# A gate's last dot products, a residual load by halves and a provisional mean in a two-layer hybrid block

## Chip, cores and metric

One core of one Trainium2 chip runs the whole block. The metric is the device time of one execution in microseconds (us); the kernel before has a median of 2440.19 us over three runs (2438.97 to 2441.34).

## What is computed

Two layers over 1024 latent tokens of width 1024 (stored as 8 tiles `d` of 128 channels). Layer 0 mixes tokens with a bidirectional RG-LRU (ten channel tiles of 128), layer 1 with a Conformer convolution module. Each layer ends in a gated ConvFFN, and every sub-layer is normed, modulated by adaLN and added to the residual h. Cut from the reference:

```python
mod = s_c @ ada_w[i] + ada_b[i]
sh1, sc1, g1, sh2, sc2, g2 = [t[:, None, :] for t in jnp.split(mod, 6, axis=-1)]
h = h + g1 * rglru_out(hf + hb, ug, w_out)          # layer 0
h = h + g1 * conformer_conv(xm, ...)                # layer 1
h = h + g2 * conv_ffn(xm2, w_up, cw, cb, w_down)    # both layers

def conformer_conv(xm, w1, b1, cw, cb, lng, lnb, w2, b2):
    a, g = jnp.split(xm @ w1 + b1, 2, axis=-1)
    v = dwconv1d(a * jax.nn.sigmoid(g), cw, cb, (15, 15))
    mu = v.mean(-1); var = ((v - mu) ** 2).mean(-1)
    return jax.nn.silu((v - mu) * rsqrt(var + EPS) * lng + lnb) @ w2 + b2

def conv_ffn(xm, w_up, cw, cb, w_down):
    v, g = jnp.split(dwconv2d(xm @ w_up, cw, cb), 2, axis=-1)
    return (jax.nn.silu(g) * v) @ w_down
```

## The kernel before

**Products and order.** Every fp32 product is made of three TensorE matmuls of a high and a low part: weights are split into `whi` (ACT) and `wlo` (mostly POOL), activations into `xmh`/`zh` (ACT) and `xml`/`zl` (DVE or POOL). A class `Order` is a list scheduler: it holds predicted durations (`dur`), a priority (`prio`, smaller first) and a sequence number, and writes one instruction order for each engine, which is then fixed; an engine runs its list strictly in that order. PE's order is the order in which the program issues matmuls. DMAs are issued by SP, in its own order, from one queue.

**Layer 0's output projection** (`rnn_out`, L1021; `k_outer`, L942). It goes by token half `hf` (512 tokens). For each half it runs over k, the ten tiles of the recurrence's output; for each k all eight output tiles d get three matmuls into eight PSUM banks. The last two k (8 and 9, `tail`) are done tile by tile with the residual add (`finish`). Each k needs a weight tile `wraw<-w_out_in` of 512 KB, with a split, and z, which `rnn_feed` reads back from DRAM (`raw<-ydr`) and `z_split` splits. During k = 4 to 7 of half 0, `load_h` (L1415) loads h, two tiles of 512 KB at each k, through the same queue.

**Layer 0's ConvFFN** (`ffn`, L1078). 22 steps p each make two column tiles of the up-projection on PE, in three PSUM pairs P0 to P2 in turn. For each tile ACT writes the centre tap and DVE adds the other eight (`ffn_conv`, `cv<-ps,vec,cv`): 16 taps, one gate product and so on per step. z of step p goes to POOL for its low part (`zl`). From p = 3 on `between()` puts a unit of the down-projection into PE's stream every four k steps: 12 matmuls into P3, then DVE adds `h<-ps,mod,h` with the gate g2 (`self.modB[l][5]`), which frees P3 for the next unit.

**The gate.** g2 of layer 0 is part 5 of `mod[0]`, eight columns, each a dot product of a row of `ada_w` with silu(c) (`ada_dot`, L543). The product of a 512 KB row tile in the two-buffer ring `raw` with `sC` is done by DVE with an accumulated sum, or by POOL with a sum on ACT. `first_tiles` issues four DVE dots at p = 0 (`prio=3`), p = 1 and p = 2 issue two POOL dots each, and then `ada_bias(0, 5)` adds the bias (`mod<-mod,vec`). `ada_dot` with a `prio` lets its load go early; with `prio=0` the load waits for `after`. Loads of the down weights (`raw<-down_in`) share the ring.

**The Conformer's layernorm** (`conformer`, L1215). Eight channel tiles; the odd ones are convolved on PE (`conv`). conv(7) is the last; its result goes to DRAM and back to be put in order again (`yt`, `cdr`, `sC`), and an ACT instruction writes CV tile 7. For half 0 `center(0, ...)` sums the mean on PE (POOL's running sum `nacc`, and CV tiles 5, 6 and 7), subtracts it from all eight tiles on DVE, squares on ACT, sums the variance on PE; then `rsqrt`, and `src` scales, applies SiLU and splits each tile for the second pointwise product. Half 1 is centred while half 0's product runs (`first` of `k_outer`), and its variance (`deviation`) is one matmul on `nacc` that stands in PE's stream behind k = 3.

Of the kernel before, what the change touches and what calls it, by code (L numbers as in the profile page):

```python
# [280 lines left out]
class Net:  # L281
# [258 lines left out]

    def ada_dot(self, l, q, eng="dve", after=(), prio=0):  # L543

        t, b = self.load_raw(self.a["ada"][l, q], after=() if prio else after)
        col, mB = self.mod[l][:, q:q + 1], self.modB[l][q // 8]
        if eng == "dve":
            self.stt(1024, t, t, 1.0, self.sC, MULT, MULT, [b, self.sCB], [b], [mB], accum=col, after=after, prio=prio)
        else:
            self.tten(1024, t, t, self.sC, MULT, [b, self.sCB], [b], eng=eng, prio=prio)  # L550
            self.act(1024, t, t, AF.Copy, [b], [b], [mB], accum=col)
# [349 lines left out]
    def k_outer(self, K, zsrc, flush, after_stat, pts=(0, 1, 2, 3), first=None, during={}, last=None):  # L901
# [30 lines left out]
        def outer(hf, after, ws):  # L932

            late = max(after) + 1 if after else 0
            for k in range(max(late, K - tail)):
                if K > 4:
                    ws[k] = self.w_next(min(2, 3 - k) if k < late else 2)
                for d in range(ND - 2 if k < late else ND):
                    unit(d, hf, [k], ws)
                    if d == (2 if K > 4 else 0) and k in after:  # L940
                        after[k](bank(ND - 1, hf))
                if hf == 0 and k in during:  # L942
                    during[k]()
                if k == late - 1:
                    for kk in range(late):
                        for d in (ND - 2, ND - 1):
                            unit(d, hf, [kk], ws)
                        if late == 4:
                            self.w_split(self.wq_use + min(kk + 1, 3))
            if K == 4:  # L950
                self.w_split(self.wq_use + 2)
                self.w_load(self.wq_use + 4)
            else:
                for k in range(K - tail, K):
                    ws[k] = self.w_next()
            for d in (0, 2, 4, 6, 1, 3, 5, 7):
                unit(d, hf, range(K - tail, K), ws)
                finish(d, hf)
# [53 lines left out]
    def rnn_feed(self, i):  # L1012

        while self.fed < min(i, 2 * NR):
            hf, k = divmod(self.fed, NR)
            t, b = self.yr.next()
            self.dma(t, self.ydr[k][:, hf * 512:hf * 512 + 512], 262144, r=[self.ydrB[k][hf]], w=[b])
            self.z_split(k, t, b, "dve")
            self.fed += 1

    def rnn_out(self, during):  # L1021
# [10 lines left out]
            b.w = [o for _, c in self.yr.items[2 * i:2 * i + 2] for o in c.w + c.r]  # L1032
            b.r = []

    def z_split(self, k, t, b, eng, n=512):
        i = self.zi % 8
        self.zi += 1
        hB, lB = self.xB[1][i]
        hi, lo = self.xmh[1][:, i, :], self.xml[1][:, i, :]
        self.act(n, hi, t, AF.Copy, [b], [hB])  # L1040
        self.tten(n, lo, t, hi.bitcast(F32), SUB, [b, hB], [lB], eng=eng, prio=-1)

    def z_slot(self, i):
        return self.xmh[1][:, i, :], self.xml[1][:, i, :], list(self.xB[1][i])
# [18 lines left out]
    def ffn(self, l, end, last=None):  # L1063
# [80 lines left out]
        for p in range(NF):  # L1144
# [9 lines left out]
            for q in ((), (0,), (1, 2))[p] if p < 3 else ():  # L1154
                quarter(0, q)
            if p == 0:
                self.first_tiles((0, 1), lambda ops: [self.ada_dot(*ada.pop(0), prio=3, after=ops) for _ in range(4)] if ada else None)
                pts, nt = [0, 1], 2
            for i, f in enumerate((p, NF + p)):
                if p:  # L1160
# [48 lines left out]
    def conformer(self, pool):  # L1209
# [56 lines left out]
        def glu(m, pt):  # L1266
# [12 lines left out]
            self.act(W, inner(hi), split(xr), AF.Copy, [xrB], [hB], prio=-2)  # L1279
            self.tten(W, inner(lo), split(xr), inner(hi).bitcast(F32), SUB, [xrB, hB], [lB], prio=-2)  # L1280

        def conv(m):
            hi, lo, hB, lB = xs[m // 2 % 2]
            out = self.P[3].rearrange("p a (b s) -> p (a b) s", b=2)
            slot = None
            for j in range(4):
                for n, d in enumerate(SHIFTS):
# [8 lines left out]
                            self.mm(out[:, j, :], w[:, c], x[:, j, s], n == 0 and q == 0, n == len(SHIFTS) - 1 and q == 2)  # L1296

                    o.pe(3 * (256 / 2400 + 0.011), go, [whB, wlB, hB, lB], [self.PB[3][j // 2]])
            for h in range(2):
                c = slice(512 * h, 512 * h + 512)  # L1300
                self.ts(512, yt[:, c], self.P[3][:, h, :], 1.0, None, MULT, None, [self.PB[3][h]], [yB[h]], prio=-2)
# [40 lines left out]
            for m in range(ND):  # L1342
                sums(m, *xs[m])

        var = self.P[1][:, 0, :]

        def sums(m, x, b):
            sq, sqB = self.tt.next()
            self.act(512, sq, x, AF.Square, [b], [sqB])
            o.pe(0.87, lambda: self.mm(var, self.ones, sq, m == 0, m == ND - 1), [self.onesB, sqB], [self.PB[1][0]])  # L1350

        center(0, (0, 0), sums)
        self.rsqrt(512, rs2[0][0], var, [self.PB[1][0]], [rs2[0][1]])

        def deviation(bank):
            ms = self.stat(*lna[1], bank)
# [7 lines left out]
        def src(hf, k):  # L1364
            while self.fed < min(hf * ND + k + 5, 16):
                h, m = order[self.fed]
                self.fed += 1
                c = slice(h * 512, h * 512 + 512)
                x, b = CV[:, m, c], cvB[m][h]
                self.tten(512, x, x, rs2[h][0], MULT, [b, rs2[h][1]], [b])  # L1370
                silu = self.act(512, x, x, AF.Silu, [b], [b], bias=self.v("cf_ln_b", m), scale=self.v("cf_ln_g", m))
                self.z_split(m, x, b, "dve")
# [29 lines left out]
    def build(self):  # L1402
        tc, o = self.tc, self.o
        with ExitStack() as main:
# [3 lines left out]
            def switch():  # L1408
# [1 line left out]
                o.drain()  # L1410
                ex.close()
                self.h = main.enter_context(tc.tile_pool(name="h", bufs=1)).tile([P, ND, 1024], F32, name="h")
                self.hB = []

            def load_h():  # L1415
                for d in (len(self.hB), len(self.hB) + 1):
                    both = Buf()
                    self.dma(self.h[:, d, :], self.a["x"][:, d, :], 524288, w=[both])
                    self.hB.append([Buf(after=[both]), Buf(after=[both])])

            during = {4: lambda: (switch(), load_h()), 5: load_h, 6: load_h, 7: load_h}
            for l in range(2):
                if l == 0:
                    self.rnn_out(during)
# [32 lines left out]
```

## Time and profile before

| | |
|---|---|
| median of 3 runs | 2440.19 us |
| profiled execution | 2438.16 us, span 2436.4 us (1.76 us lie around the span) |
| granted TensorE clock, mean | 0.979 |
| PE busy | 2326.2 us, 95% |
| DVE busy | 1896.6 us, 78% |
| ACT, POOL busy | 967.3 us (40%), 798.1 us (33%) |
| DMA | 214.98 MB, mean 88 GB/s |

In the profile a time is a position in the span, in us; "released by" or "<-" names the engine and tile whose end ended a wait. A matmul record is longer than the step from one to the next, since matmuls are pipelined. A granted clock of 1.0 is the 2.4 GHz level, 0.5 the 1.2 GHz level.

### The profile page before, as it was taken

To read this page: it belongs to the slowest core of one execution; us is meant where nothing else is said; L and a number is where in the kernel's file an instruction comes from. 1 tells how busy PE (TensorE), PEld (TensorE's weight loads), DVE (VectorE), ACT (ScalarE), POOL (GpSimd) and SP (SyncE) were. 2 spreads that over 40 slices of the span, in tenths; PEclk is the share of its full clock that TensorE was granted. 3 is DMA by queue.
4 is the path that set the end of the run, shared out by engine and by line. 5 is a ranking of instruction groups with operands and counts; after the bars stand their busy time and mean duration, and the time that the engine had idled before them with its cause. 6 is when DMAs were issued, how large, how long until landed. Compare 5 with 4: busy or idle time off the path is not lost.

```text
span 2436.4 us, 26124 instructions
## 1 busy us (share of the span) xinstructions
PE 2326.2 (95%) x10440; PEld 1892.8 (78%) x10440; DVE 1896.6 (78%) x1752; ACT 967.3 (40%) x1141; POOL 798.1 (33%) x409
## 2 busy tenths in 40 slices
PE   7999999889789999999999999889999999999997
PEld 2788888667578888888887888667888888888886
DVE  6677877776867777777878898677997777777878
ACT  4577777544233333333324333365322221222223
POOL 1100000354345544554523233245333322332323
PEclk9999999899899999999999999899999999999999
DMA  6324325253132323223211233422111111111101
GB/s 262 120 84 144 94 84 162 96 198 117 55 101 95 104 87 104 95 88 103 91 35 36 66 114 105 138 70 91 52 58 52 44 39 52 52 52 48 44 26 70
DMA packets 82442, 214.98 MB, mean 88 GB/s; under 512 B 8528, under 2 KB 33104, under 8 KB 82192
## 3 DMA queue, kind: packets, MB, share of 16 engines
q1 hardware_dynamic: 80448, 210.68, 26.3%
q10 hardware_dynamic: 1872, 2.62, 0.3%
q8 instruction: 82, 1.34, 0.2%
q14 instruction: 40, 0.33, 0.0%
HBM read 192.10 MB, written 13.63 MB: 84 GB/s over the span
## 4 chain that ended last, share of the span: by engine, by line
PE 70%; DVE 16%; ACT 5%; issue 3%; DMA 2%; POOL 2%; SPq 0%; ACTq 0%; DVEq 0%; POOLq 0%
PE ps L441 70%; DVE cv L362 4%; DVE CV L362 3%; DVE F L770 1%; ACT F L354 1%; POOL wlo L369 1%; DVE F L362 1%; DVE tt L362 1%; DVE F L369 1%; DVE rs L384 1%; ACT tt L354 1%; DVE raw L362 1%; ACT L354 1%; DVE h L362 1%; ACT whi L354 1%
## 5 line engine op out<-in xcount | busy, mean ns | idle before, releaser
L362 DVE SCALAR_TENSOR_TENSOR cv<-ps,vec,cv 128x960 f32<-128x960 f32 (+2 forms) x720 | 861.5, 1198 | 203.6 <-ACT cv L354 185.2
L441 PE MATMUL ps<-xmh,whi 128*128 128x512 f32 x2272 | 744.5, 394 | 19.7 <-ACT xmh L354 8.9
L441 PE MATMUL ps<-xmh,wlo 128*128 128x512 f32 x2272 | 738.0, 392 | 9.5 <-POOL wlo L369 5.9
L441 PE MATMUL ps<-xml,whi 128*128 128x512 f32 x2272 | 740.5, 393 | 4.6 <-DVE xml L362 4.2
L369 POOL TENSOR_TENSOR wlo<-wraw,whi 128x1024 fp32r<-128x1024 f32 (+1 forms) x164 | 399.8, 2442 | 712.6 <-ACT whi L354 694.9
L441 PEld LDWEIGHTS ps<-xmh,whi 128*128 128x128 f32 x2272 | 427.8, 189 | 115.9 <-ACT xmh L354 12.0
L441 PEld LDWEIGHTS ps<-xmh,wlo 128*128 128x128 f32 x2272 | 429.4, 189 | 103.1 <-POOL wlo L369 7.9
L441 PEld LDWEIGHTS ps<-xml,whi 128*128 128x128 f32 x2272 | 429.8, 189 | 102.4 <-DVE xml L362 9.4
L362 DVE SCALAR_TENSOR_TENSOR h<-ps,mod,h 128x1024 f32<-128x1024 f32 (+2 forms) x216 | 231.5, 1080 | 61.0 <-PE ps L441 60.8
L354 ACT ACTIVATE whi<-wraw 128x1024 fp32r<-128x1024 f32 (+1 forms) x198 | 205.2, 1042 | 123.3 <-PE ps L441 51.5
L354 ACT ACTIVATE cv<-ps,vec 128x1024 f32<-128x1024 f32 (+1 forms) x90 | 105.9, 1181 | 299.5 <-PE ps L441 280.5
L369 POOL TENSOR_TENSOR zl<-cv,zh 128x1024 fp32r<-128x1024 f32 x42 | 101.2, 2411 | 350.6 <-ACT zh L354 350.6
L441 PE MATMUL ps<-zh,dnh 128*128 128x512 f32 x576 | 180.1, 393 | 23.0 <-DVE h L362 23.0
L369 POOL TENSOR_TENSOR raw<-raw,sC 128x1024 f32<-128x1024 f32 x52 | 125.1, 2406 | 178.7 <-DMA raw<-ada_in 174.0
L441 PE MATMUL ps<-zl,dnh 128*128 128x512 f32 x576 | 181.4, 397 | 0.0
L441 PE MATMUL ps<-zh,dnl 128*128 128x512 f32 x576 | 177.8, 390 | 0.0
L354 ACT ACTIVATE raw<-raw 128x1024 f32<-128x1024 f32 x52 | 55.2, 1062 | 289.4 <-POOL raw L369 289.4
L354 ACT ACTIVATE cv<-cv 128x1024 f32<-128x1024 f32 (+1 forms) x46 | 47.0, 1022 | 293.5 <-DVE cv L362 293.3
L369 POOL TENSOR_TENSOR dnl<-raw,dnh 128x512 fp32r<-128x512 f32 x72 | 94.0, 1307 | 202.5 <-ACT dnh L354 202.5
L362 DVE SCALAR_TENSOR_TENSOR CV<-ps,vec,CV 128x1009 f32<-128x1009 f32 (+14 forms) x120 | 153.1, 1275 | 8.6 <-ACT CV L354 4.9
L441 PEld LDWEIGHTS ps<-zh,dnh 128*128 128x128 f32 x576 | 108.6, 189 | 45.9 <-DVE h L362 23.4
L441 PEld LDWEIGHTS ps<-zh,dnl 128*128 128x128 f32 x576 | 108.4, 188 | 26.4
(141 smaller groups left out, 2414.6 us busy)
## 6 DMA issues: line engine op xcount, KB each, us to landing
raw<-ada_in SPq DMA_DIRECT2D x88, 512.0 KB, 4.2
wraw<-up_in SPq DMA_DIRECT2D x88, 512.0 KB, 3.3
raw<-down_in SPq DMA_DIRECT2D x72, 256.0 KB, 3.2
wraw<-w_in SPq DMA_DIRECT2D x32, 512.0 KB, 3.3
wraw<-w_in_in SPq DMA_DIRECT2D x20, 512.0 KB, 3.9
wraw<-w_out_in SPq DMA_DIRECT2D x20, 512.0 KB, 3.7
wraw<-cw_in SPq DMA_DIRECT2D x16, 512.0 KB, 3.6
wraw<-gw_in SPq DMA_DIRECT2D x10, 512.0 KB, 3.4
```

Source lines behind the costliest of these rows:

```text
L354: "act", 0.21 + n * 0.00083, lambda: self.nc.scalar.activation(out, in_, func, **kw),
L362: lambda: self.nc.vector.scalar_tensor_tensor(out=out, in0=in0, scalar=scalar, in1=in1, op0=op0, op1=op1, **kw),
L369: return self.o.op(eng, dur, lambda: e.tensor_tensor(out=out, in0=in0, in1=in1, op=op), r, w, wp, prio=prio)
L384: return self.o.op("dve", 0.07 + n * 0.0063, lambda: self.nc.vector.reciprocal(out=out, in_=in_), r, w)
L441: self.nc.tensor.matmul(out, w, x, start=start, stop=stop)
L770: lambda t=t, a=a, ig=ig, rev=rev: nc.vector.tensor_tensor_scan(rev(t), rev(a), rev(ig), 0.0, op0=MULT, op1=ADD),
```

## The change

Four edits. (1) `ada_dot` takes the early load as a parameter of its own, and the four dots of `first_tiles` get `prio=0` in place of 3. (2) `load_h` loads h by token halves: 256 KB for each tile, half 0 at the same k as before, half 1 at k = 0 to 3 of half 1. (3) The first four `z_split` of `rnn_feed` get a priority of 4 (and 3 for the low part). (4) For half 0 of the Conformer's layernorm the mean of the first seven tiles is summed inside conv(7); `deviate` subtracts 8/7 of it on DVE from each tile and squares the result on ACT; when tile 7 has come back, one matmul on its deviation gives the difference d between the provisional and the true mean, the variance is corrected by d squared, and d is subtracted from every tile in `src`, one more DVE instruction per tile.

```diff
-    def ada_dot(self, l, q, eng="dve", after=(), prio=0):
-        t, b = self.load_raw(self.a["ada"][l, q], after=() if prio else after)
+    def ada_dot(self, l, q, eng="dve", after=(), prio=0, early=False):
+        t, b = self.load_raw(self.a["ada"][l, q], after=() if early else after)
...
-                if hf == 0 and k in during:
-                    during[k]()
+                if (hf, k) in during:
+                    during[hf, k]()
...
-            self.z_split(k, t, b, "dve")
+            self.z_split(k, t, b, "dve", prio=4 if self.fed < 4 else 0)
...
-                self.first_tiles((0, 1), lambda ops: [self.ada_dot(*ada.pop(0), prio=3, after=ops) for _ in range(4)] if ada else None)
+                self.first_tiles((0, 1), lambda ops: [self.ada_dot(*ada.pop(0), early=True, after=ops) for _ in range(4)] if ada else None)
...
+        def provisional():
+            parts = [lna[0], *((CV[:, m, :512], cvB[m][0]) for m in LATE[:-1])]
+            for i, (t, tB) in enumerate(parts):
+                o.pe(0.87, lambda: self.mm(self.P[0][:, 1, :], self.ones, t, i == 0, i == len(parts) - 1), [self.onesB, tB], [self.PB[0][1]])
...
+                    if m == ND - 1 and j == 3 and n == 5:
+                        provisional()
...
-        var = self.P[1][:, 0, :]
-
-        def sums(m, x, b):
+        r, rB = rs2[0]
+        d, dB = lna[0]
+        (mp, mpB), (mu, muB), (var, varB) = [(self.P[i][:, j, :], self.PB[i][j]) for i, j in ((0, 1), (0, 0), (1, 0))]
+
+        def total(out, outB, t, tB, first, last):
+            o.pe(0.87, lambda: self.mm(out, self.ones, t, first, last), [self.onesB, tB], [outB])
+
+        def deviate(m, y, yB):
+            self.stt(512, y, mp, -ND / (ND - 1.0), CV[:, m, :512], MULT, ADD, [cvB[m][0], mpB], [yB], prio=-3)
             sq, sqB = self.tt.next()
-            self.act(512, sq, x, AF.Square, [b], [sqB])
-            o.pe(0.87, lambda: self.mm(var, self.ones, sq, m == 0, m == ND - 1), [self.onesB, sqB], [self.PB[1][0]])
-
-        center(0, (0, 0), sums)
-        self.rsqrt(512, rs2[0][0], var, [self.PB[1][0]], [rs2[0][1]])
+            self.act(512, sq, y, AF.Square, [yB], [sqB], prio=-4)
+            return sq, sqB
+
+        for m in range(ND - 1):
+            total(var, varB, *deviate(m, CV[:, m, :512], cvB[m][0]), m == 0, False)
+        w, wB = vt[:, :512], vB
+        sq = deviate(ND - 1, w, wB)
+        total(mu, muB, w, wB, True, True)
+        total(var, varB, *sq, False, True)
+        sq, sqB = self.tt.next()
+        self.act(512, sq, mu, AF.Square, [muB], [sqB], prio=-4)
+        self.act(512, d, mu, AF.Copy, [muB], [dB], prio=-3)
+        self.tten(512, r, var, sq, SUB, [varB, sqB], [rB], prio=-4)
+        self.rsqrt(512, r, r, [rB], [rB])
+        inverse = list(rB.w)
...
+                if h == 0:
+                    x, b = (w, wB) if m == ND - 1 else (x, b)
+                    o.op("dve", 0.72, lambda x=x: nc.vector.tensor_tensor(out=x, in0=x, in1=d, op=SUB), [b, dB], [b], after=inverse if m else ())
...
-            def load_h():
-                for d in (len(self.hB), len(self.hB) + 1):
-                    both = Buf()
-                    self.dma(self.h[:, d, :], self.a["x"][:, d, :], 524288, w=[both])
-                    self.hB.append([Buf(after=[both]), Buf(after=[both])])
-
-            during = {4: lambda: (switch(), load_h()), 5: load_h, 6: load_h, 7: load_h}
+            def load_h(hf, d0):
+                for d in (d0, d0 + 1):
+                    c = slice(hf * 512, hf * 512 + 512)
+                    self.dma(self.h[:, d, c], self.a["x"][:, d, c], 262144, w=[self.hB[d][hf]])
+
+            during = {(hf, 4 * (1 - hf) + i): lambda hf=hf, i=i: load_h(hf, 2 * i) for hf in range(2) for i in range(4)}
+            during[0, 4] = lambda: (switch(), load_h(0, 0))
```

**The gate's dots, DVE, start of layer 0's ConvFFN.** Names: `cv<-ps,vec,cv` is a tap (or a few of one form), `raw_77,mod_92<-raw_77,sC` a dot, `mod_92<-mod_92,vec` the gate's bias, `h<-ps_68,mod_92,h` a unit's add to h. Before, where the fourth dot stands:

```order
L362 SCALAR_TENSOR_TENSOR cv_3480<-ps_66,vec,cv_3480 128x15x63 x4
L362 SCALAR_TENSOR_TENSOR cv_3481<-ps_67,vec,cv_3481 128x960 x2
L362 SCALAR_TENSOR_TENSOR cv_3481<-ps_67,vec,cv_3481 128x16x63 x2
L362 SCALAR_TENSOR_TENSOR cv_3481<-ps_67,vec,cv_3481 128x15x63 x4
L362 SCALAR_TENSOR_TENSOR raw_77,mod_92<-raw_77,sC 128x1024
L369 TENSOR_TENSOR cv_3480<-cv_3480,cv_3481 128x1024
L369 TENSOR_TENSOR mod_92<-mod_92,vec 128x8
L362 SCALAR_TENSOR_TENSOR h<-ps_68,mod_92,h 128x1024 x2
```

and now, from the third dot on:

```order
L362 SCALAR_TENSOR_TENSOR raw_76,mod_92<-raw_76,sC 128x1024
L362 SCALAR_TENSOR_TENSOR cv_3487<-ps_65,vec,cv_3487 128x960 x2
L362 SCALAR_TENSOR_TENSOR raw_77,mod_92<-raw_77,sC 128x1024
L362 SCALAR_TENSOR_TENSOR cv_3487<-ps_65,vec,cv_3487 128x16x63 x2
L362 SCALAR_TENSOR_TENSOR cv_3487<-ps_65,vec,cv_3487 128x15x63 x4
L362 SCALAR_TENSOR_TENSOR cv_3488<-ps_66,vec,cv_3488 128x960 x2
L362 SCALAR_TENSOR_TENSOR cv_3488<-ps_66,vec,cv_3488 128x16x63 x2
L362 SCALAR_TENSOR_TENSOR cv_3488<-ps_66,vec,cv_3488 128x15x63 x4
L362 SCALAR_TENSOR_TENSOR cv_3489<-ps_67,vec,cv_3489 128x960
L369 TENSOR_TENSOR cv_3487<-cv_3487,cv_3488 128x1024
L362 SCALAR_TENSOR_TENSOR cv_3489<-ps_67,vec,cv_3489 128x960
L369 TENSOR_TENSOR mod_92<-mod_92,vec 128x8
```

The fourth dot stood behind the 48 taps of the first six tiles and now stands behind two; the gate's bias stood behind all 48 and now stands behind 18, and the first two adds to h, which stood together behind it, now lie four and five tiles' taps in (not shown).

**The Conformer's layernorm, DVE, from conv(7)'s result on.** Names: `yt` is conv(7)'s result on its way to DRAM, `CV<-CV,ps_65` the old centring, `CV<-ps_65,CV` the provisional one, `nacc_89` at L1397 is d, `CV<-CV,rs` the scaling of half 0, `CV<-CV,ps_68` the centring of half 1. Before:

```order
L377 TENSOR_SCALAR yt<-ps_68 128x512 x2
L369 TENSOR_TENSOR CV<-CV,ps_65 128x512 x8
L384 RECIPROCAL rs<-rs 128x512
L369 TENSOR_TENSOR CV<-CV,rs 128x512 x4
L369 TENSOR_TENSOR xml_75<-CV,xmh_73 128x512 x2
L369 TENSOR_TENSOR CV<-CV,rs 128x512
L369 TENSOR_TENSOR xml_75<-CV,xmh_73 128x512 x3
L369 TENSOR_TENSOR CV<-CV,ps_68 128x512 x3
```

and now:

```order
L377 TENSOR_SCALAR yt<-ps_68 128x512
L362 SCALAR_TENSOR_TENSOR CV<-ps_65,CV 128x512
L377 TENSOR_SCALAR yt<-ps_68 128x512
L362 SCALAR_TENSOR_TENSOR CV<-ps_65,CV 128x512 x6
L362 SCALAR_TENSOR_TENSOR raw_76<-ps_65,CV 128x512
L369 TENSOR_TENSOR rs<-ps_66,tt 128x512
L1397 TENSOR_TENSOR CV<-CV,nacc_89 128x512
L384 RECIPROCAL rs<-rs 128x512
L369 TENSOR_TENSOR CV<-CV,rs 128x512
L1397 TENSOR_TENSOR CV<-CV,nacc_89 128x512
L369 TENSOR_TENSOR CV<-CV,rs 128x512
L1397 TENSOR_TENSOR CV<-CV,nacc_89 128x512
```

Seven centrings moved ahead of tile 7's return, one of them between the two copies of `yt`; seven of the eight subtractions of d stand behind the reciprocal, in turn with the scalings, and ahead of or among half 1's centring.

## Rows read from the trace of the kernel before

**Rows 1.** The page, part 4: the chain that ended last, by engine.

```profile
PE 70%; DVE 16%; ACT 5%; issue 3%; DMA 2%; POOL 2%; SPq 0%; ACTq 0%; DVEq 0%; POOLq 0%
```

**Rows 2.** PE's waits: line waited for, us in total, times, longest us.

```profile
PE ps L441 <- DVE h L362: 26.5, 4, 23.0
```

**Rows 3.** Windows: stretch, length, then busy us (instructions) of PE, PEld, DVE, ACT, POOL, clock, DMA share, GB/s.

```profile
650.00:660.00 10.00, 3.16 (x14) 2.27 (x13) 9.74 (x10) 1.06 (x1) 0.00 (x0) 0.81 0.00 0
660.00:670.00 10.00, 0.00 (x0) 0.00 (x0) 0.79 (x1) 2.21 (x3) 4.63 (x2) 0.50 0.28 95
670.00:680.00 10.00, 3.85 (x9) 3.07 (x10) 1.45 (x2) 3.82 (x5) 3.61 (x2) 0.50 0.26 88
680.00:690.00 10.00, 10.00 (x45) 8.17 (x45) 8.79 (x8) 1.58 (x2) 6.87 (x4) 0.99 0.51 160
```

**Rows 4.** Timeline, DVE and POOL near 600: start, length, what, count, idle before and releaser.

```profile
596.41 21.08 DVE L362 SCALAR_TENSOR_TENSOR cv<-ps,vec,cv 128x960 f32<-128x960 f32 x17
598.18 2.40 POOL L369 TENSOR_TENSOR wlo<-wraw,whi 128x1024 fp32r<-128x1024 f32 x1 [7.89 <-ACT whi L354]
```

**Rows 5.** Timeline, all engines, 650 to 678.

```profile
649.61 8.77 DVE L362 SCALAR_TENSOR_TENSOR cv<-ps,vec,cv 128x960 f32<-128x960 f32 x7
...
658.30 1.22 DVE L362 SCALAR_TENSOR_TENSOR raw<-raw,sC 128x1024 f32<-128x1024 f32 x1
```

**Rows 6.** The chain in order of time, 660 to 680: start, us, what.

```profile
667.80 3.13 DMA raw<-ada_in
...
670.99 2.35 POOL raw L369
...
674.82 1.29 DVE h L362
...
676.15 4.15 PE ps L441 x9
```

**Rows 7.** SP's issues of the four tiles of ada_w, near 575.

```profile
575.67 19.14 SPq L343 DMA_DIRECT2D raw<-ada_in  x4
```

**Rows 8.** The page, part 6, DMA issues: count, KB each, median us to landing.

```profile
raw<-ada_in SPq DMA_DIRECT2D x88, 512.0 KB, 4.2
```

**Rows 9.** Window in layer 0's output projection, columns as in rows 3.

```profile
490.00:500.00 10.00, 4.56 (x13) 2.45 (x12) 4.88 (x3) 3.15 (x4) 4.70 (x2) 0.79 1.03 406
```

**Rows 10.** SP's issues of h ahead of the last weight tile of half 0.

```profile
482.96 0.89 SPq L343 DMA_DIRECT2D h<-x_in  x2
...
484.86 1.30 SPq L343 DMA_DIRECT2D h<-x_in  x2
```

**Rows 11.** The chain in order of time, 478 to 500.

```profile
486.20 9.29 DMA wraw<-w_out_in
...
496.73 2.36 POOL wlo L369
```

**Rows 12.** Timeline, PE, in the Conformer's layernorm.

```profile
1561.45 1.02 PE L441 MATMUL ps<-nacc,ones 128*128 128x512 f32 x2
1562.31 1.88 PE L441 MATMUL ps<-CV,ones 128*128 128x512 f32 x4
...
1589.64 0.79 PE L441 MATMUL ps<-xmh,whi 128*128 128x512 f32 x1 [6.40 <-ACT xmh L354]
...
1612.26 1.12 PE L441 MATMUL ps<-nacc,ones 128*128 128x512 f32 x2 [1.88 <-POOL nacc L369]
```

**Rows 13.** Timeline, DVE, in the same stretch.

```profile
1573.05 4.87 DVE L369 TENSOR_TENSOR CV<-CV,ps 128x512 f32<-128x512 f32 x8 [10.11 <-PE ps L441]
1584.00 3.35 DVE L384 RECIPROCAL rs<-rs 128x512 f32<-128x512 f32 x1 [6.08 <-ACT rs L354]
...
1599.94 0.68 DVE L369 TENSOR_TENSOR CV<-CV,rs 128x512 f32<-128x512 f32 x1
...
1601.82 2.88 DVE L369 TENSOR_TENSOR nacc<-nacc,tt 128x512 f32<-128x512 f32 x1
```

**Rows 14.** Timeline, POOL, beside it.

```profile
1601.75 2.40 POOL L369 TENSOR_TENSOR wlo<-wraw,whi 128x1024 fp32r<-128x1024 f32 x1
```

More of the change, by code (lines that the diff above doesn't have):

```diff
@@ L1033, in rnn_out, with z_split @@
             b.r = []
-    def z_split(self, k, t, b, eng, n=512):
+    def z_split(self, k, t, b, eng, n=512, prio=0):
         i = self.zi % 8
@@ L1039, in z_split @@
         hi, lo = self.xmh[1][:, i, :], self.xml[1][:, i, :]
-        self.act(n, hi, t, AF.Copy, [b], [hB])
-        self.tten(n, lo, t, hi.bitcast(F32), SUB, [b, hB], [lB], eng=eng, prio=-1)
+        self.act(n, hi, t, AF.Copy, [b], [hB], prio=prio)
+        self.tten(n, lo, t, hi.bitcast(F32), SUB, [b, hB], [lB], eng=eng, prio=prio - 1)
     def z_slot(self, i):
@@ L1412, in switch @@
                 self.h = main.enter_context(tc.tile_pool(name="h", bufs=1)).tile([P, ND, 1024], F32, name="h")
-                self.hB = []
-            def load_h():
-                for d in (len(self.hB), len(self.hB) + 1):
-                    both = Buf()
-                    self.dma(self.h[:, d, :], self.a["x"][:, d, :], 524288, w=[both])
-                    self.hB.append([Buf(after=[both]), Buf(after=[both])])
-            during = {4: lambda: (switch(), load_h()), 5: load_h, 6: load_h, 7: load_h}
+                self.hB = [[Buf(), Buf()] for _ in range(ND)]
+            def load_h(hf, d0):
[4 more added lines that the diff above has]
+            during[0, 4] = lambda: (switch(), load_h(0, 0))
             for l in range(2):
```

## Prediction

> **What bounds the kernel now.** I read the chain of waits first. PE holds 70% of it [rows 1], so a change counts only where PE stands still or where something else ends a stretch of PE's work. The list of PE's waits then names the largest hole by far: 26.5 us in four waits for DVE's add to h, one of them 23.0 us long [rows 2]. The windows place it: PE works 3.16 us of the ten from 650, none from 660 to 670, 3.85 us from 670 to 680, and is full again after that [rows 3]. What the reader is to see in the next two views is why. DVE is full until 658 with taps (17 in 21.08 us [rows 4], 7 in 8.77 us [rows 5]: 1.24 us each), and only then comes `raw<-raw,sC` at 658.30, the fourth of the gate's early dots [rows 5]. Its data had been asked for by 594.8, as the last of the four issues that began at 575.67 and took 19.14 us [rows 7]. So the dot did not wait for data; it stood behind 48 taps in DVE's order. It holds one of the two `raw` buffers, the next loads wait for that buffer, and the rest follows one link after another: load at 667.80, POOL's product at 670.99, the sum on ACT, the gate's bias, the add to h at 674.82, PE at 676.15 [rows 6]. The second unit of the down-projection cannot enter P3 before that add has emptied it.
>
> Two smaller holes lie where the change also works: the tail of layer 0's output projection, where PE works 4.56 us of the ten from 490 [rows 9], and the Conformer's layernorm, where PE waits 6.40 us up to 1589.64 and 1.88 us up to 1612.26 [rows 12].
>
> **The change, part by part.** Edits are costed against the profiled execution, 2438.16 us, which is 2.03 us under the median of 2440.19.
>
> *The gate's dots.* Nothing is added; one dot of 1.22 us moves ahead of 46 taps. In the new order it comes after two taps, at about 596.41 + 2 x 1.24 = 598.9. Its load, issued by 594.8, lands about 4.2 us later [rows 8], near 599.0: the two meet, and DVE waits nothing or a few tenths. The dots that depend on the buffer then start some 35 us earlier; the order puts the gate's bias behind 18 taps, about 596.4 + 18 x 1.24 + 1.2 for the dot and 1.2 for a gate product = 621. The first add to h then hangs on P3 alone. I place it among the taps of the fifth tile, near 649 to 650, so the second unit enters P3 near 653, where PE stopped before. Is something else late next? DVE's backlog is the candidate. PE runs ahead of DVE by about one step: by my walk along both orders the taps of the sixth tile end near 662.4, and PE needs that bank for its ninth tile only near 672, 9.5 us later. Nearer is POOL's low part of z for the first unit: with DVE 1.2 us later it is ready near 645.75, wanted near 646.3. From step 3 on a step gives DVE about 25.5 us (16 taps, products and three or four adds) and PE about 32.7 us, so the backlog shrinks. So the whole 23.0 us goes. With it goes the slow clock behind it: from 670 to 680 the clock is 0.50, the 1.2 GHz level, and the 9 matmuls took 3.85 us; at 45 in 10.00 us [rows 3] they would take 2.0. Term: **−23.0 − 1.85 = −24.85 us**. Bounds: 0 if the gate is as late as before; the same −24.85 as the most.
>
> *h by halves.* The queue is full from 490 on (DMA share 1.03 at 406 GB/s [rows 9]). Ahead of the last weight tile of half 0, issued at 486.20, stand four h loads [rows 10]; each shrinks by 262,144 bytes, together 1.05 MB, 2.58 us at 406 GB/s. That tile's 9.29 us end at 495.49, its split on ACT and POOL follows at once and ends at 499.09 [rows 11], and PE goes on. 2.58 us sooner its split would meet POOL still busy with the tile before, but two of the four loads stand ahead of that one too, so it comes about 1.3 us sooner and POOL is free in time. I take **−2.6 us**. Bounds: 0, if the z parts that ride in the same queue end last instead; −5.4, the whole idle time of the ten us from 490 [rows 9]. The eight loads of half 1 run beside 40 us of PE's work and are wanted only by that half's adds; I cost them at nothing, and if they came late it would be those adds and the norm behind them.
>
> *Priority of the first splits.* One split on ACT changes places with four others while PE is in the recurrence; the first product needs all of them later. Nothing.
>
> *The provisional mean.* Three matmuls move into conv(7), 0.86 us each (1561.45 to 1562.31 [rows 12]), so conv(7) ends 2.58 us later, and one centring of 0.66 stands between the two copies of `yt`: tile 7 comes back 3.25 us later. Behind it there are no longer eight centrings (4.87 us [rows 13]) and a row of squares, but one centring, one square, two short sums and a subtraction. I get the reciprocal at 1579.15 in place of 1584.00 [rows 13], and the product's first matmul near 1584.75 in place of 1589.64 [rows 12]: 4.9 us won. Then it is given back. DVE now carries seven more subtractions of about 0.61 us behind the reciprocal, 4.3 us, on the way to half 1's sum of squares, which PE waits for at 1612.26 [rows 12]. From the reciprocal's start to that point it was 28.2 us; now 32.5, plus a little for the order: about 1611.9. PE arrives 4.9 us sooner than before and waits about 6.4 us where it waited 1.88. The trace of before shows what a restart behind a long gap costs, 1.85 us in the term above [rows 3]; whether a gap of 6.4 us is long enough it does not show at this place. I take the full price: −0.3 + 1.85 = **+1.55 us**. Bounds: −4.9, if the sum of squares keeps its lead; +5, if the subtractions add their full 4.9 and the lead is lost.
>
> POOL bears on this. Beside POOL's `wlo` of 2.40 us at 1601.75 [rows 14] a DVE instruction with both inputs in SBUF took 2.88 us, where one of that size takes 0.68 [rows 13]; the taps, with one input in PSUM, keep their 1.24 us beside POOL [rows 4] and without it [rows 5]. The subtractions of d have both inputs in SBUF; the centrings they follow had one in PSUM. But POOL is idle between 1584 and 1600, so only the last two or three can meet it. The Trainium skill, *SBUF — State Buffer*, section "SBUF: two separate sides", has the rule: DVE and GpSimd take one shared port pair as an exclusive lock, whoever comes second is blocked for the whole instruction, and a DVE instruction with two SBUF inputs is among those that need it. By that rule the change turns cheap centrings into instructions that can be locked out, and with one hit more the term would be about +3.75 instead of +1.55; the trace agrees with it at 1601.82, where the hit was 2.2 us.
>
> **Sum.** −24.85 − 2.6 + 1.55 = −25.9; 2438.16 gives 2412.3 for a profiled execution, and the median 2440.19 gives **2414.3**.
>
> **Rivals.**
> - *DVE's backlog takes over.* For it: DVE is 97% busy from 650 to 660 [rows 3], the low part of z has half a microsecond to spare, and the adds to h now compete with taps. Against: 9.5 us to spare at the ninth tile. If PE waits at each of the next units, I take a third to a half of the hole back, 8 to 12 us: 2422 to 2426. Chance 0.13.
> - *More than forecast.* Half 1's sum of squares keeps its lead (6.45 us better), or the tail's whole gap closes (2.8 better), or both: 2405 to 2411.5. For it: the walk at the layernorm rests on DVE alone. Chance 0.17.
> - *A lock more.* Two or three subtractions of d meet POOL and lose 2.88 − 0.68 = 2.2 us each [rows 13], 4.4 to 6.6, with half 1's sum of squares waiting behind them: 2419 to 2421. For it: they are of the kind that was held at 1601.82. Against: POOL is idle while most of them run. Chance 0.08. (The lock is the one that the Trainium skill's page states.)
> - *The gate is as late as ever*, since another link of its chain (a POOL product behind weight splits) holds it: the first term is 0 and the rest −1.05: 2439. Chance 0.04.
> - *Slower.* The fourth dot now stands in front of 46 taps. If its load lands late, DVE stands, and with it every tap. Each us beyond the spare half becomes a us of PE's. It decides once the load is later than 599 by more than 24.85 + 1.05 + 4.9, some 31 us: over 2445. The row against it is the 4.2 us of 88 such loads [rows 8]. Chance 0.02.
>
> The forecast itself has 0.56.
>
> **Range and chances.** The forecast's own width is about ±4 us. The range from 2404 to 2426 takes in that, the better case, the lock and the backlog, and leaves out the last two. A measurement of this kernel can tell 0.2%, 4.9 us, from no change. Faster: 0.94; the same: 0.04; slower: 0.02.
>
> **What would show it.** Right: no PE wait above a few us between 640 and 690 and a clock near 1.0 there; the dot near 599, the bias near 621; the last weight tile of half 0 landing about 2.6 us sooner; the layernorm's reciprocal about 5 us sooner against conv(7)'s place, and a PE wait of about 6 us for half 1's sum. Wrong: a wait for DVE or POOL of over 5 us at the next units, the bias still behind the taps, or no wait at half 1's sum. All later positions move up by what was won before them.

## The result, and the profile after

| | before | changed |
|---|---|---|
| median | 2439.58 us (4 runs) | 2422.04 us (4 runs, 2420.78 to 2422.86) |
| ratio, 95% interval | | 0.9928, 0.9911 to 0.9946 |
| span of the profiled execution | 2436.4 us | 2420.7 us |

The change is faster by 17.5 us (13 to 22 by the interval). The range held it; the point, 25.9 us less, was 8 us too much.

The chain that ended last in the changed kernel (page, part 4) is more PE than before [rows 1]:

```profile
PE 80%; DVE 10%; ACT 4%; DMA 1%; issue 1%; POOL 1%; SPq 0%; ACTq 0%; DVEq 0%; POOLq 0%
```

PE's waits in the changed kernel (line waited for, us in total, times, longest us), against [rows 2]:

```profile
PE ps L441 <- ACT xmh L354: 9.0, 4, 7.2
...
PE ps L441 <- POOL nacc L369: 6.0, 1, 6.0
...
PE ps L441 <- ACT dnh L354: 2.9, 1, 2.9
...
PE ps L441 <- DVE h L362: 1.9, 4, 0.9
```

The 23.0 us for DVE's add to h are gone. New are 6.0 us for half 1's sum (`POOL nacc`), 2.9 us put down to the split of a down weight (`ACT dnh`), and 2.6 us for tile 7's deviation (`DVE raw`, its row stands further down). The 7.2 us for `ACT xmh` are the wait before the product, 6.40 us before [rows 12]. The windows at the place of the old hole, to be read against [rows 3]:

```profile
600.00:610.00 10.00, 7.12 (x32) 5.59 (x31) 9.79 (x10) 6.14 (x8) 8.51 (x4) 1.00 0.50 163
...
650.00:660.00 10.00, 10.00 (x46) 8.22 (x45) 9.86 (x9) 1.84 (x2) 2.31 (x2) 1.00 0.17 54
660.00:670.00 10.00, 10.00 (x45) 8.24 (x44) 9.17 (x9) 3.08 (x3) 3.34 (x2) 1.00 0.17 52
670.00:680.00 10.00, 10.00 (x45) 8.26 (x44) 9.82 (x9) 2.89 (x4) 6.35 (x4) 1.00 0.33 122
```

PE is full from 650 on, at the 2.4 GHz level. The dip is now between 600 and 610, 7.12 us of ten. There DVE's timeline of the changed kernel shows the dot in its new place [rows 4, 5]:

```profile
595.71 2.46 DVE L362 SCALAR_TENSOR_TENSOR cv<-ps,vec,cv 128x960 f32<-128x960 f32 x2
598.09 2.88 DVE L362 SCALAR_TENSOR_TENSOR raw<-raw,sC 128x1024 f32<-128x1024 f32 x1
...
621.74 0.15 DVE L369 TENSOR_TENSOR mod<-mod,vec 128x8 f32<-128x8 f32 x1
```

and the timelines of POOL and PE what lies beside it and what follows:

```profile
597.48 2.40 POOL L369 TENSOR_TENSOR wlo<-wraw,whi 128x1024 fp32r<-128x1024 f32 x1 [7.89 <-ACT whi L354]
...
608.55 0.70 PE L441 MATMUL ps<-xmh,whi 128*128 128x512 f32 x2 [2.88 <-ACT dnh L354]
```

The gate is ready at 621.7, as forecast. The dot took 2.88 us and not 1.22: POOL's weight part had begun 0.6 us before it. DVE's remaining six taps of the first tile then end at about 600.9 + 6 x 1.24 = 608.3, and PE starts its fourth tile, in the same PSUM pair, at 608.55. Before, the same start waited 0.21 us:

```profile
606.58 0.70 PE L441 MATMUL ps<-xmh,whi 128*128 128x512 f32 x2 [0.21 <-DVE cv L362]
```

**Three stretches.** For every kernel I cut PE's 10,440 matmul records at the same six records, and read the windows between. The three rows are: from the output projection's last k through the change of halves; the first tiles of layer 0's ConvFFN through the old hole; the Conformer's layernorm and the product behind it. Before, and the third stretch of the same kernel in a second profile (run e9, below), whose first two took 70.40 and 93.40 us:

```profile
451.59:523.88 72.29, 64.55 (x262) 51.03 (x260) 52.13 (x37) 32.93 (x40) 32.43 (x13) 0.93 0.56 199
601.68:695.42 93.74, 70.53 (x301) 57.49 (x300) 71.25 (x61) 28.05 (x33) 38.02 (x18) 0.87 0.23 76
1542.51:1699.90 157.39, 133.62 (x573) 102.07 (x572) 104.97 (x111) 87.92 (x114) 67.45 (x33) 0.93 0.29 92
```

```profile
1540.90:1698.54 157.64, 133.54 (x573) 102.14 (x571) 104.96 (x111) 87.93 (x114) 67.87 (x33) 0.94 0.28 92
```

The changed kernel, first profile, and the third stretch of its second (run e10), whose first two took 70.03 and 71.32 us:

```profile
451.75:523.17 71.42, 65.18 (x261) 50.83 (x260) 55.04 (x38) 32.57 (x40) 32.38 (x13) 0.93 0.57 193
600.98:672.29 71.31, 68.43 (x302) 56.23 (x301) 68.70 (x58) 26.41 (x31) 36.87 (x18) 1.00 0.29 92
1518.64:1684.24 165.60, 138.68 (x572) 105.54 (x571) 109.68 (x120) 89.60 (x117) 69.82 (x33) 0.91 0.28 89
```

```profile
1518.36:1683.87 165.51, 138.62 (x573) 105.54 (x571) 109.83 (x120) 89.71 (x117) 69.79 (x33) 0.91 0.27 89
```

The second column is the length. In these four profiles the first stretch scatters by up to 1.9 us within a kernel, and the other two repeat within 0.4 us; e2 and e11 below, which are one kernel, do not repeat so well. So: first stretch −0.6 us (means 71.35 to 70.73), second −22.3 (93.57 to 71.32), third **+8.0** (157.5 to 165.55). Together −14.9; the spans of these four profiles differ by 15.2.

### The profile page after: what moved, and what is told of

Its sections match the earlier page's. It is cut to its first block, busy times and chain, and to the rows that moved or that the text cites. A ratio compares the mean times of both kernels' runs of the same rounds, so it can differ in the third digit from the quotient of the medians.

```text
span 2420.7 us, 26147 instructions
## 1 busy us (share of the span) xinstructions
PE 2330.0 (96%) x10440; PEld 1894.2 (78%) x10440; DVE 1907.1 (79%) x1761; ACT 967.5 (40%) x1143; POOL 798.5 (33%) x409
## 4 chain that ended last, share of the span: by engine, by line
PE 80%; DVE 10%; ACT 4%; DMA 1%; issue 1%; POOL 1%; SPq 0%; ACTq 0%; DVEq 0%; POOLq 0%
PE ps L441 80%; DVE cv L362 1%; ACT F L354 1%; DVE tt L362 1%; DVE F L770 1%; DVE F L362 1%; DVE rs L384 1%; DVE F L369 1%; ACT L354 1%; POOL wlo L369 1%; DVE h L362 1%; DVE xml L362 1%; ACT tt L354 1%; DVE raw L362 1%; DVE nacc L369 1%
## 5 line engine op out<-in xcount | busy, mean ns | idle before, releaser
L441 PEld LDWEIGHTS ps<-zl,dnh 128*128 128x128 f32 x576 | 107.9, 187 | 24.6
```

Of the source, the lines that this page charges most:

```text
L441: self.nc.tensor.matmul(out, w, x, start=start, stop=stop)
```

## The experiments

Each run is set against runs of the kernel before on the same chip. Rows are PE's timeline where nothing else is said.

**e1, the gate's dots alone.** The kernel before with the two lines of the first edit:

```diff
-... self.ada_dot(*ada.pop(0), prio=3, after=ops) ...
+... self.ada_dot(*ada.pop(0), early=True, after=ops) ...
```

> The kernel before with the gate's dots alone changed (first edit). Theory 1: the hole of 23.0 us and its slow clock go (-24.9 us), but the fourth dot, now ahead of six taps of the first tile, holds up PSUM pair P0, which PE's fourth tile waits for with no slack (0.21 us of wait before); that costs 2.9 us, so the run takes 24.9 - 2.9 = 22.0 us less than the kernel before, about 2418, and PE waits 2.5 to 3 us at the fourth tile, near 606. Rival: the dot's move is free, as the prediction had it: 24.9 us less, about 2415, and no wait there.

Measured: 2421.22 us against 2440.93, ratio 0.9916 (0.99 to 0.9932), 19.7 us less. The interval, 16.6 to 24.4 us, holds the 22.0 of theory 1 and leaves out the rival's 24.9. At the fourth tile:

```profile
609.18 1.19 PE L441 MATMUL ps<-xmh,whi 128*128 128x512 f32 x2 [2.88 <-DVE cv L362]
```

The wait is there again, 2.88 us, and here the profile puts it down to the taps (`DVE cv`). Theory 1 holds for the wait. The second stretch took 74.16 us, 2.8 more than in the changed kernel, with a mean clock of 0.95 where the changed kernel had 1.00: in this execution a stretch at the 1.2 GHz level followed the wait. So it did in e11 (74.12 us, 0.95), but not in e2 (71.28 us, 1.00), the same kernel.

**e2, the layernorm of before.** The changed kernel with `conformer` as it was.

> The changed kernel with the layernorm of before (edits 1 to 3 stay). Theory 1: the provisional mean as changed costs 8 us in all, so this run is 8 us faster than the changed kernel, about 2414. Rival: the layernorm costs 1.55 us as predicted and the shortfall lies in the first part of the program: 2420 to 2421.

Measured: 2417.82 us against 2440.93, ratio 0.9907 (0.989 to 0.9923), 23.1 us less, where the changed kernel had 17.5 less. The layernorm edit costs some 5 us: neither 8 nor 1.55. The windows of the third stretch say why both missed (this run, then its second profile, e11):

```profile
1514.91:1676.18 161.27, 136.16 (x573) 102.17 (x571) 102.83 (x111) 87.77 (x114) 66.79 (x33) 0.92 0.28 90
```

```profile
1519.84:1682.31 162.47, 137.68 (x572) 104.75 (x571) 104.88 (x111) 88.00 (x114) 68.91 (x33) 0.91 0.28 90
```

The old layernorm took 157.4 and 157.6 us in the kernel before, and 161.3 and 162.5 here. PE's busy time is 2.5 to 4 us longer for the same matmuls, at a lower mean clock.

**e3, the dot behind the first tile's taps.** As e2; the dot is issued when the first tile's eight taps are, and waits for them.

```diff
+                if held:
+                    held.pop()(list(accB.w))
```

> As the run without the layernorm edit, with the fourth dot's load where it is and the dot itself behind all eight taps of the first tile. Theory 1: the wait at PE's fourth tile falls from 2.9 to under 0.5 us, the later hole stays closed, and the run is 2.5 us faster than the run without the layernorm edit, about 2411.5. Rival: the wait there is for ACT (as the list of waits names it, the split of a down weight), so it stays near 2.9 us and nothing is won.

Measured: 2416.34 us against 2440.93, ratio 0.9903 (0.9888 to 0.9918). It can't be told from e2. The wait did not go; it moved to the next two tiles, and 1.65 + 1.02 + 0.21 is 2.88 us again:

```profile
603.83 0.70 PE L441 MATMUL ps<-xmh,whi 128*128 128x512 f32 x2 [0.21 <-DVE cv L362]
...
616.61 0.70 PE L441 MATMUL ps<-xmh,whi 128*128 128x512 f32 x2 [1.65 <-DVE cv L362]
...
628.75 0.70 PE L441 MATMUL ps<-xmh,whi 128*128 128x512 f32 x2 [1.02 <-DVE cv L362]
```

Both readings fall: ACT is not what PE waits for, and the first tile is not the only one with little slack. The dot met POOL's next weight part here, 603.04 to 605.43, and took 2.91 us (DVE):

```profile
603.60 2.91 DVE L362 SCALAR_TENSOR_TENSOR raw<-raw,sC 128x1024 f32<-128x1024 f32 x1
```

**e5, the dot on POOL.** So the theory was changed: PE waits for DVE through the first six tiles, and whatever DVE is given there is paid in full. As e2, with

```diff
-... self.ada_dot(*ada.pop(0), early=True, after=ops) for _ in range(4)] ...
+... self.ada_dot(*ada.pop(0), eng, early=True, after=ops) for eng in ("dve", "dve", "dve", "pool")] ...
```

> As the run without the layernorm edit, with the fourth dot on POOL (product) and ACT (sum) in place of DVE, its load unchanged. Theory 1: in the first six tiles PE waits for DVE's taps with no slack, so any instruction added to DVE there is paid in full; the dot on DVE costs 2.9 us (1.2 its own, 1.7 behind POOL's weight part), wherever it stands among the taps. Without it the wait of 2.9 us goes, the hole stays closed, and the run is 2.9 us faster than the run without the layernorm edit. Rival: three POOL products in a row push the next weight part back, PE waits 1 to 3 us for it at the fifth tile, and nothing is won.

Measured: PE's wait at the fourth tile, then the second stretch:

```profile
604.47 0.70 PE L441 MATMUL ps<-xmh,whi 128*128 128x512 f32 x2 [0.27 <-ACT raw L354]
```

```profile
599.51:668.26 68.75, 68.48 (x302) 56.18 (x300) 66.88 (x56) 27.81 (x33) 38.20 (x19) 1.00 0.28 96
```

0.27 us is left of 2.88, and the stretch is 2.55 us shorter than in the changed kernel; 93.57 − 68.75 = 24.8 us is what the hole was worth, the forecast's 24.85. The whole run, 2415.44 us against 2438.23, ratio 0.9903 (0.9889 to 0.9918), is not told apart from e2's: in this profile the third stretch took 162.3 us, and the runs of one kernel scatter by as much as is to be shown.

**e7, h by halves alone.** The kernel before with the second edit.

> The kernel before with h by halves alone (second edit). Theory 1: the tail's four waits of 5.5 us fall to about 3.5, the wait for DVE's add to h at the change of halves (2.3 us) to under 1, and a new wait of about 2 us appears at half 0's sum of squares, which did not come sooner: 1.5 to 2 us less than before in that stretch. Rival: the prediction's 2.6 us, all of it kept, with no wait at the sum of squares.

Measured over 10 runs: 2436.32 us against 2438.23, ratio 0.9994 (0.9985 to 1.0004): not told from no change. The first stretch took 71.04 us; over all profiles it took 71.6 on average without the edit (4 profiles, 70.40 to 72.29) and 70.4 with it (9 profiles, without e8, 69.02 to 71.42), so about −1.2 us, with groups that overlap. Before, PE's waits in the tail and at the change of halves were

```profile
492.21 0.50 PE L441 MATMUL ps<-xmh,whi 128*128 128x512 f32 x1 [0.97 <-ACT whi L354]
494.63 0.50 PE L441 MATMUL ps<-xmh,wlo 128*128 128x512 f32 x1 [1.70 <-POOL wlo L369]
496.70 0.79 PE L441 MATMUL ps<-xmh,whi 128*128 128x512 f32 x1 [1.57 <-ACT whi L354]
499.13 0.80 PE L441 MATMUL ps<-xmh,wlo 128*128 128x512 f32 x1 [1.21 <-POOL wlo L369]
515.82 0.50 PE L441 MATMUL ps<-xmh,whi 128*128 128x512 f32 x1 [2.30 <-DVE h L362]
```

and here those of theory 1:

```profile
492.35 0.50 PE L441 MATMUL ps<-xmh,wlo 128*128 128x512 f32 x1 [1.53 <-POOL wlo L369]
493.15 0.50 PE L441 MATMUL ps<-xmh,whi 128*128 128x512 f32 x1 [0.30 <-ACT whi L354]
495.58 0.79 PE L441 MATMUL ps<-xmh,wlo 128*128 128x512 f32 x1 [1.69 <-POOL wlo L369]
511.44 0.50 PE L441 MATMUL ps<-xmh,whi 128*128 128x512 f32 x1 [0.41 <-DVE h L362]
517.17 1.45 PE L441 MATMUL ps<-nacc,ones 128*128 128x512 f32 x2 [2.04 <-DVE nacc L369]
```

The tail's waits are 3.5 us in place of 5.45; but PE then stands 2.04 us at half 0's sum of squares, and the 4.63 us from there to the end of the stretch run at a mean clock of 0.63, where before 2.93 us ran at 1.00.

**e8, that sum one k later.** As e5, with the sum behind k = 2 in half 1 of the output projection:

```diff
-            outer(1, {1: after_stat}, ws)
+            outer(1, {stat_k: after_stat}, ws)
```

> As the run with the dot on POOL, and half 0's sum of squares in the output projection stands one k later in PE's stream (behind the third product of k = 2). Theory 1: PE has 18 matmuls, 4 us, more to do before it, so the wait of 2.0 us there goes and the run is about 2 us faster than the run with the dot on POOL. Rival: the norm that follows is late by 4 us too, and the first up-projection tiles wait for it: the same time or slower.

Measured: 2410.44 us against 2438.23, ratio 0.9886 (0.987 to 0.9902), the fastest kernel here that leaves nothing out, 27.8 us below the kernel before. Against e5's 2415.44 the runs overlap (2408.14 to 2416.11, and 2414.47 to 2416.99). No wait for `nacc` is left in the stretch, which took

```profile
453.55:519.77 66.22, 62.21 (x261) 49.79 (x260) 52.09 (x36) 30.78 (x37) 32.54 (x13) 0.97 0.53 184
```

4.2 us less than e5's 70.41. Some 0.7 of it is the sum itself, which now lies behind the cut: from the first stretch's start to the second's it is 144.70 us against e5's 148.22, 3.5 less. That is more than the 2.04 us of the wait; the mean clock is 0.97 where e5 had 0.95. Against e2 and e3, with clocks of 0.98 and 0.97, the same distance is 2.3 and 2.2 us shorter (146.98 and 146.86), about the wait itself. The rival's wait did not come: the first up-projection tiles cost PE the same 1.2 us for DVE's low parts as in e5.

**e6, no subtraction of d.** The changed kernel without the line at L1397. It leaves out the correction from the provisional to the true mean.

> The changed kernel without the eight subtractions of d (the correction of the mean is left out, all else stays). Theory 1: they are what half 1's sum of squares waits behind: from the product's first matmul to that sum 22.5 to 23.5 us in place of 27.2, PE's wait there 1 to 2 us in place of 6.0, and 4.5 to 7 us off the changed kernel, 2415 to 2417.5. Rival: the loss comes of the gaps ahead of the product (tile 7's way through DRAM with a slow clock); then the stretch up to the sum stays near 27 us and the time within 1 us of the changed kernel's.

Measured: 2410.75 us against 2438.23, ratio 0.9879 (0.9863 to 0.9896), 27.5 us less, 10 more than the changed kernel and more than theory 1's 4.5 to 7; the profiled execution, at 2414.26 us, is the slowest of the four. Its product's first matmul and half 1's sum, then the same two in the changed kernel:

```profile
1563.15 0.79 PE L441 MATMUL ps<-xmh,whi 128*128 128x512 f32 x1 [7.23 <-ACT xmh L354]
1586.20 1.99 PE L441 MATMUL ps<-nacc,ones 128*128 128x512 f32 x2 [1.90 <-POOL nacc L369]
```

```profile
1564.08 0.80 PE L441 MATMUL ps<-xmh,whi 128*128 128x512 f32 x1 [7.23 <-ACT xmh L354]
...
1591.24 2.08 PE L441 MATMUL ps<-nacc,ones 128*128 128x512 f32 x2 [6.04 <-POOL nacc L369]
```

23.05 us in place of 27.16, and 1.90 us of wait in place of 6.04: the subtractions are what the sum waits behind. The third stretch took 158.2 us, 7.4 less: 0.4 of it ahead of the product, 4.1 from there to the sum, and 2.9 behind the sum, where 90.13 us at a mean clock of 0.98 stand in place of 93.00 at 0.95.

**e4, subtractions on POOL.** The changed kernel, with the subtractions of tiles 2 to 7 on POOL; the second tile's, on DVE, no longer waits for the reciprocal.

> The changed kernel with five of the eight subtractions of d (tiles 2 to 6) and tile 7's on POOL, which is idle from 1557 to 1575 there; the first two stay on DVE. Theory 1: DVE's subtractions are what holds half 1's sum of squares back, so PE's wait for that sum falls from 6.0 to about 2 us and the slow clock behind it goes, 4 + 2.9 = about 7 us faster than the changed kernel, 2415. Rival: POOL's subtractions take the lock that DVE's scalings need, so DVE loses as much as it is spared: 2420 to 2424 and a wait of 5 to 7 us.

Measured: 2418.29 us against 2440.93, ratio 0.9907 (0.989 to 0.9925), 22.6 us less, 5 more than the changed kernel; between the two. Both happen:

```profile
1566.14 0.79 PE L441 MATMUL ps<-xmh,whi 128*128 128x512 f32 x1 [10.08 <-ACT xmh L354]
1589.82 1.16 PE L441 MATMUL ps<-nacc,ones 128*128 128x512 f32 x2 [3.46 <-POOL nacc L369]
```

The wait at the sum is 2.6 us shorter, the wait ahead of the product 2.85 longer, since the two subtractions left on DVE, 1.3 us of work, took 3.52 us beside POOL's weight part and the first of POOL's own subtractions, which began at 1558.21, and held up the reciprocal. DVE, then POOL:

```profile
1556.95 3.52 DVE L369 TENSOR_TENSOR CV<-CV,nacc 128x512 f32<-128x512 f32 x2
```

```profile
1555.90 2.35 POOL L369 TENSOR_TENSOR wlo<-wraw,whi 128x1024 fp32r<-128x1024 f32 x1 [10.49 <-ACT whi L354]
```

**e9 to e11, three kernels profiled again,** for the third stretch.

> The kernel before once more, for its profile. In its first profile the stretch from 1542.5 to 1699.9 (the Conformer's layernorm and the product behind it) took 157.4 us; with the same layernorm code and the gate's dots changed it took 159.8 to 162.3 in five profiles. Theory 1: that is how the clock falls in one execution or another, so this profile lies anywhere from 157 to 162. Rival: it belongs to the kernel, and this profile gives 157.4 within half a us.

> The changed kernel once more. Its first profile took 165.6 us for the same stretch. Theory 1: waits alike (7.2 us before the product, 6.0 us at half 1's sum), the stretch 162 to 167 as the clock falls. Rival: 165.6 within half a us. At the fourth tile of layer 0's ConvFFN both expect the wait of 2.9 us again.

> The run without the layernorm edit once more. Its first profile took 161.3 us for the stretch. Theory 1: 157 to 163, as the clock falls. Rival: 161.3 within half a us, since the code before it sets how the clock falls.

Measured: 157.64, 165.51 and 162.47 us (rows above); whole executions of 2436.53, 2422.02 and 2419.99 us. The kernel before and the changed one repeat within 0.3 us, as the rivals said, the third within 1.2 only, against its rival; and all three lie in theory 1's ranges, so that these three alone settle nothing. The groups do. With the gate's hole closed the old layernorm's stretch takes 159.8 to 162.5 us in six profiles (e1, e2, e3, e5, e8, e11; mean 161.3); with the hole open 157.4 to 157.8 in three (before, e7, e9). The groups do not overlap: the longer stretch goes with the closed hole.

**e12, the layernorm alone.** The kernel before with the fourth edit.

> The kernel before with the layernorm edit alone (fourth edit). In profiles the stretch from conv(7)'s end part on took 157.4 to 157.8 us with the old layernorm and the hole of 23 us ahead of it, 159.8 to 162.5 with the old layernorm and the hole closed, 165.5 and 165.6 with the new one and the hole closed. Theory 1: the two add up, so the new layernorm behind the hole takes 157.6 + 4.2 = about 162 and the run is 3 to 6 us slower than the kernel before. Rival: the new layernorm costs 8 us by itself, 165.5 here too, and the run is 7 to 9 us slower.

Measured: 2442.9 us against 2441.13, ratio 1.0008 (0.9999 to 1.0018); the third stretch:

```profile
1541.27:1703.28 162.01, 137.98 (x573) 104.92 (x572) 109.78 (x120) 88.99 (x116) 67.47 (x33) 0.92 0.28 89
```

162.0 us, 4.5 more than the 157.5 of before: the stretch is what theory 1 gave, and the two effects add up (157.5 + 4.5 + 3.8 = 165.8 against 165.5). The whole time, +1.8 us with an interval of −0.2 to +4.4, is below theory 1's 3 to 6; that the edit alone slows the kernel is shown in the stretch and not by the whole time.

## Why the prediction was right, and where it was off

| step | forecast | found | from |
|---|---|---|---|
| gate's dots | −24.85 | −22.3 | second stretch; −19.4 in e1 and e11, −24.8 without the dot on DVE |
| h by halves | −2.6 | −1.2 | first stretch, 13 profiles |
| provisional mean | +1.55 | +4.3 | third stretch: 165.55 − 161.3, and 4.5 in e12 |
| not in the sum | 0 | +3.8 | third stretch, old layernorm: 161.3 − 157.5 |
| sum | −25.9 | −15.4 | profiles; −17.5 by the medians |

The range held the time because it had been widened for the rivals: 2422.04 us lies outside the forecast's own ±4 us, and where the first rival had been put. All four rows miss the same way, so no error made good for another.

*The gate's dots.* Right in mechanism, place and price: the hole was the dot's place in DVE's order, the gate was ready at 621.7 (forecast 621), and closing the hole was worth 24.8 us with its slow clock. The step that failed is "the taps of the sixth tile end near 662.4, and PE needs that bank ... 9.5 us later" as the place to look for slack, with "the spare half" microsecond of POOL's z as the nearest. Slack was asked for behind the move and not at it. PE's fourth tile already waited 0.21 us for the first tile's taps, so there was next to none, and e3 leaves about 1.3 us at the fifth tile (2.91 − 1.65) and 0.2 at the sixth (1.02 less again). The dot took 2.88 us and not 1.22, since it met POOL's weight part; the first rival's mechanism, DVE as the bound, thus came true, at the tiles rather than at the units.

*The dot and the lock.* The row of 1601.82 [rows 13, 14] had priced this, and the prediction applied it to the layernorm alone. The dot too has both inputs in SBUF, and the place forecast for it, 598.9, lay inside the weight part that [rows 4] show on POOL, 598.18 to 600.58. The Trainium skill, *SBUF — State Buffer*, section "SBUF: two separate sides", says that a DVE instruction with two SBUF inputs waits for the whole GpSimd instruction ahead of it, if that one reads SBUF, as the weight part does. The rows agree: 2.88 us at 598.09 (POOL until 599.88), 2.91 at 603.60 in e3 (POOL until 605.43), each ending about 1.1 us behind POOL, which is near its own 1.22.

*h by halves.* The link itself came true: the split of half 0's last weight tile began 2.5 us sooner (493.27 − 451.75 = 41.52 us behind the stretch's start, before 495.60 − 451.59 = 44.01). On the average of the 4 and the 9 profiles the tail's waits fell from 5.0 to 3.1 us and that at the change of halves, which was not counted, from 2.3 to 1.0. But half 0's sum of squares, behind DVE, did not come sooner by as much, and PE waited 2.0 us there: 1.9 + 1.3 − 2.0 = 1.2. The step that failed is the one left out: what is late next. The walk ended at "and PE goes on". e8 shows the price by taking that wait away. The loads of half 1 cost nothing that shows, as forecast.

*Priority of the first splits.* It has no run of its own; that it costs nothing is not shown by itself.

*The provisional mean.* The forecast named the give-back, and e6 shows it: "DVE now carries seven more subtractions" on the way to half 1's sum, PE waiting "about 6.4 us" (6.04 measured). The sizes are seen best in e12, which has the old hole ahead of it as the forecast's rows had. From the start of the stretch (1541.27 there, 1542.51 before) the product came 3.7 us sooner and not 4.9 (1584.70 − 1541.27 = 43.43, before 47.13 [rows 12]), and half 1's sum 0.8 later and not 0.3 sooner (1611.85 − 1541.27 = 70.58, before 69.75). The step that failed most is the last term, the restart behind the wait, "1.85 us in the term above": from the sum to the end of the stretch, before and in e12,

```profile
1612.26:1699.90 87.64, 83.52 (x358) 66.82 (x359) 60.01 (x60) 52.49 (x68) 47.05 (x22) 1.00 0.25 84
```

```profile
1611.85:1703.28 91.43, 88.11 (x358) 69.66 (x359) 57.26 (x59) 50.62 (x66) 46.33 (x22) 0.95 0.24 81
```

the same matmuls took 3.8 us more at a mean clock of 0.95 in place of 1.00 (the changed kernel: 93.00 us at 0.95). The clock was 0.70 in the ten us behind the sum and 1.00 there before; in e12 it fell once more, to 0.85, in the ten us from 1651.85, and how much of the 3.8 us belongs to which was not separated. 0.8 + 3.8 is the 4.6 us by which e12's stretch is longer than the first profile's of before.

In the changed kernel the reciprocal came 1.7 us sooner than before (1584.00 − 1542.51 = 41.49; 1558.43 − 1518.64 = 39.79) and not 4.85, because tile 7 was back 5.6 us later and not 3.25 (its first instruction 34.04 and 28.43 us behind the start), and its two sums ran mostly at the 1.2 GHz level behind the gap (mean clock 0.56):

```profile
1553.43 2.07 PE L441 MATMUL ps<-raw,ones 128*128 128x512 f32 x2 [2.64 <-DVE raw L362]
1555.29 1.55 PE L441 MATMUL ps<-tt,ones 128*128 128x512 f32 x2
```

where [rows 12] had 1.02 us for two. The third rival happened too, at half its price: a scaling and two subtractions met POOL's sums (1575.00, 1580.14 and 1585.14, 1.4 to 1.6 us each) and took 1.0 to 1.1 us more than their usual 0.68 to 0.69 (DVE, changed kernel):

```profile
1575.50 1.67 DVE L369 TENSOR_TENSOR CV<-CV,rs 128x512 f32<-128x512 f32 x1
...
1580.52 1.78 DVE L1397 TENSOR_TENSOR CV<-CV,nacc 128x512 f32<-128x512 f32 x1
...
1585.34 1.75 DVE L1397 TENSOR_TENSOR raw<-raw,nacc 128x512 f32<-128x512 f32 x1
```

*What was in no step.* 3.8 us were given back in code that the first edit doesn't touch: with the hole 850 us ahead of it closed, the old layernorm's stretch is longer, as the nine profiles show. The waits before the product (6.40 us) and at half 1's sum (1.88 to 1.92) are alike in all nine. What differs is mostly PE's busy time for the same matmuls, 133.5 to 133.8 us with the hole open and 134.7 to 138.0 with it closed, at mean clocks of 0.93 to 0.94 and 0.91 to 0.93. Why the clock falls otherwise there was not settled; e2 and e11, one kernel, differ in it too (1.00 and 0.70 in the stretch's first ten us).

## What to carry to other kernels

When an instruction is moved forward in an engine's order, look for slack first at the next buffer that this engine frees, not some steps on: a wait of 0.2 us there meant that the move was paid for almost in full (2.55 of 2.88 us), and then another engine is the place for it. An instruction on DVE with both inputs in SBUF is to be priced with POOL's work beside it, and a transfer that comes sooner is followed to the next thing that PE waits for. A wait that grows is to be priced with the clock behind it, and a row from another place is only a first guess at that (1.85 us taken, 3.8 found). A correction that is put off from the head of a chain to its tail is worth something only if the tail's engine has room for it.

## What the runs showed that was not expected

The stretch around the layernorm repeats within 0.3 us in two profiles of the kernel before and of the changed kernel, parts at the 1.2 GHz level included (within 1.2 us in e2 and e11), and yet the same code differs by 3.8 us on average between kernels that differ only 850 us and more ahead of it. The output projection, by contrast, scatters by 2 us from profile to profile of one kernel (72.29 and 70.40).
